# Low halves of weight blocks and of the gated output: from VectorE and GpSimd to VectorE alone

## The chip, the cores and the metric

The kernel runs on one core of a Trainium2 chip. Its engines each take their own instructions in a fixed order: TensorE (PE; its weight loads are listed as PEld), VectorE (DVE), ScalarE (ACT), GpSimd (POOL) and SyncE (SP), which here issues the DMAs. The metric is the device time of one execution in microseconds; the time of a kernel is the median over its runs.

## The reference

The reference is a decoder trunk of two layers on 2048 tokens of width 1024, all in float32. Cut to what matters:

```python
# layer A: gated MLP with causal mixing inside chunks of 128 tokens
u, v, z = split(h @ w_in, 3)                 # each 2048 wide
v = rms_norm(gelu(v), sgu_g)
mixed = einsum(tril(w_s), v) + b_s
y = gelu(u) * mixed * silu(z)                # the gated output
x = x + gate * (y @ w_out)
# shared k and v of three dilation groups (1, 4, 16)
k, v = split(h_kv @ w_kv, 2);  k = rms_norm(k, k_norm_g)
# layer B: dilated sliding-window attention, 24 query heads, three groups
q, z = split(h_b @ w_in_b);    q = rms_norm(q) * 128 ** -0.5
o = softmax-weighted sum over the groups of attention(q_g, k_g, v_g)
x = x + gate * ((o * silu(z)) @ w_out_b)
```

Each `h` is an RMS norm of x with a scale and shift computed from a conditioning vector.

## The kernel before

**Two halves of a number.** TensorE is fed a rounded format (`float32r`). To keep the precision, each operand is held as a high half, which is the rounded value, and a low half, which is the value less the high half. A product takes three matmuls: high by high, high by low, low by high (`mm3`, L262). So each weight block, 128 rows by 512 columns, is loaded raw by DMA, copied to its high half by ACT (L242) and subtracted to its low half (L246). The function `split` (L240) does this and chooses the engine of the subtraction: POOL where the caller says `pool`, or where a running count of blocks `wcnt` modulo `share[0]` is 3; else DVE. `wunits` (L248) makes the blocks of a dense product, `dense_f` (L285) those of the products whose output has features on the partitions. Raw blocks lie in 6 buffers, split ones in 8; a buffer comes free when its last reader is done, and SP issues loads in order.

**Stages.** The tokens are worked in four quarters of 512 (`for Q in range(NQ)`, L1197). Per quarter, `layer_A` (L648) computes v (four blocks of 512 columns, `dense`), u and z (eight blocks of 256 columns each, `dense_f`), and the output projection (`dense` over `yT`, L720). As z's blocks are done, L685 to L690 take silu, multiply into the gated output y, copy y's high half on ACT (L689) and subtract its low half (L690). `norm_T2` (L462) then makes the normalised, transposed operands of what follows; L715 to L717 compute each row's norm before it (L233 and L234 on POOL between them). `proj_B` (L738) computes shared k and v (`kv_block`, three blocks of 8 weight blocks), and q of three groups and layer B's z (`q_block`, `z_block`) with a Strassen scheme of seven products of four weight blocks each (`dense_s`, L361); L386 adds up the products on DVE. L780 to L783 norm q on POOL, and L785 stores it. `make_ops` (L487) makes the Strassen operands, with their low halves in turn on POOL and DVE (L496).

The weight blocks of one quarter are 32 for v, 32 for u, 32 for z, 32 for the output projection, 24 for kv and 112 for q and z of layer B. In `begin` (L580), which does the first v block of the first quarter, 8 blocks are made with `ordered=True`, which puts their low halves on POOL.

**Side work.** Attention of a quarter's blocks (`attend`, L1013, steps `att_1` to `att_4`) and other small work run as generators in a list `fillers`; `tick` (L84), called after each weight block of a dense product, advances them at `rate[0]` steps a tick, so their instructions lie between those of the dense products. `share[0]` is 4 at the start, is set very large at L1196 before the quarters begin, and back to 4 at L694, behind layer A's z of the first quarter. On POOL attention has the steps L941 to L944, L968 and L1043. `finish` (L1048) makes 16 weight blocks of its own whose low halves are subtracted on POOL at L1058.

**Order.** A planner of the framework orders each engine's instructions when the program is built, from the order of the source, the dependences and its own estimates of durations; only loads in `wunits` with `ordered` and what stands in `issue_after` are pinned. An engine waits in order: an instruction whose input isn't ready holds back all behind it.

Of the kernel before, what the change touches and what calls it, by code (L numbers as in the profile page):

```python
# [12 lines left out]
F32 = mybir.dt.float32  # L13
F32R = mybir.dt.float32r
AF = mybir.ActivationFunctionType
ALU = mybir.AluOpType
# [18 lines left out]
def trunk(ctx, tc, out, x, c, a_ada_w, a_ada_b, a_norm_g, a_w_in, a_sgu_g, a_w_spatial,  # L35
          a_b_spatial, a_w_out, kv_ada_w, kv_ada_b, kv_norm_g, w_kv, k_norm_g, b_ada_w,
          b_ada_b, b_norm_g, b_w_in, b_q_norm_g, b_w_out, dbg=None):
    nc = tc.nc
# [43 lines left out]
    rate = [0, 0]  # L82
# [11 lines left out]
    def evt(name, dt=F32):  # L94
        return ep.tile([P, 512], dt, tag="ev", name=name)

    def pst(name, tag="a"):
        return ps.tile([P, 512], F32, tag=tag, name=name)
# [126 lines left out]
    def bcast(src, nm):  # L225
        t = bp.tile([P, 512], F32, tag="bc", name=nm)
        nc.sync.dma_start(t, src.broadcast_to([P, 512]))
        return t


    def rstd_of(ssq, n, width, nm):
        t = sp.tile([P, 16], F32, tag="rs", name=nm)
        nc.gpsimd.tensor_scalar(t[:, 0:n], ssq, 1.0 / width, EPS, ALU.mult, ALU.add)  # L233
        nc.gpsimd.tensor_tensor(t[:, 0:n], t[:, 0:n], mhalf[:, 0:n], ALU.pow)  # L234
        return t

    wcnt = [0]
    share = [4]
# [27 lines left out]
    def dense(hs, w, n0, nm, evac):  # L266

        pts = {}
        for kh, (hh, hl) in enumerate(hs):
            us = wunits(w, kh * KT, n0, f"{nm}_{kh}_")  # L270
            for pr in range(2):
                for t in (2 * pr, 2 * pr + 1):
                    if kh == 0:
                        pts[t] = pst(f"pd_{nm}_{t}", "d")
                for k in range(KT):
                    for t in (2 * pr, 2 * pr + 1):
                        sl = slice(t * P, (t + 1) * P)
                        mm3(pts[t], hh[:, k, sl], hl[:, k, sl], us[k],
                            kh == 0 and k == 0, kh == len(hs) - 1 and k == KT - 1)
                    tick(0.25)  # L280
                if kh == len(hs) - 1:
                    for t in (2 * pr, 2 * pr + 1):
                        evac(t, pts[t])

    def dense_f(hh, hl, w, n0, nm, evac):  # L285

        pts = [pst(f"pd_{nm}_{i}", "d") for i in range(2)]
        for kk in range(0, KT, 4):
            for j in range(0, 4, 2):
                u = wp.tile([P, 2, 2, 256], F32R, tag="w", name=f"w_{nm}{kk + j}")  # L290
                raw = rp.tile([P, 2, 256], F32, tag="raw", name=f"raw_{nm}{kk + j}")
                nc.sync.dma_start(
                    raw, w[(kk + j) * P:(kk + j + 2) * P, n0:n0 + 256].rearrange("(k p) n -> p k n", p=P))
                split(u[:, 0], u[:, 1], raw)
                for k in (kk + j, kk + j + 1):
                    for i in range(2):
                        wh = u[:, 0, k % 2, i * P:(i + 1) * P]
                        wl = u[:, 1, k % 2, i * P:(i + 1) * P]
                        nc.tensor.matmul(pts[i], wh, hh[:, k, :], start=k == 0, stop=False)  # L299
                        nc.tensor.matmul(pts[i], wh, hl[:, k, :], start=False, stop=False)  # L300
                        nc.tensor.matmul(pts[i], wl, hh[:, k, :], start=False, stop=k == KT - 1)  # L301
                    tick(0.25)
        for i in range(2):
            evac(i, pts[i])
# [109 lines left out]
    def bigr(nm):  # L414
        return big.tile([P, KT, QT], F32R, tag="big", name=nm)
# [40 lines left out]
    def new_ops(nm):  # L456

        t = [big.tile([P, 2, 2, 4, 256], F32R, tag="big", name=f"ho{nm}{i}") for i in range(4)]
        return {n: (t[i // 2][:, i % 2, 0], t[i // 2][:, i % 2, 1])
                for i, n in enumerate(("11", "12", "22", "s1", "s2", "s3", "s4"))}  # L460
# [107 lines left out]
    def v_evac(Q, m, sqv, j):  # L568
        def ev(t, pt):
            mb = m[j // 2][:, t, (j % 2) * 512:(j % 2 + 1) * 512]  # L570
            nc.scalar.activation(mb, pt, AF.Gelu_apprx_tanh)
            jk = evt(f"jk{Q}_{j}_{t}")
            nc.scalar.activation(jk, mb, AF.Square, accum_out=sqv[t][:, j:j + 1])
        return ev
# [73 lines left out]
    def layer_A(Q, hA, m, sqv, j0):  # L648
        for j in range(j0, 4):
            dense([hA], a_w_in, AW + j * 512, f"v{Q}{j}", v_evac(Q, m, sqv, j))  # L650
        for t in range(TPQ):
            nc.vector.tensor_reduce(sqv[t][:, 15:16], sqv[t][:, 0:4], AX.X, ALU.add)
            rv = rstd_of(sqv[t][:, 15:16], 1, AW, f"rv{Q}_{t}")
            for h in range(2):
                nc.vector.tensor_scalar(m[h][:, t, :], m[h][:, t, :], rv[:, 0:1], None, ALU.mult)
        mt = [big.tile([P, KT, QT], F32, tag="big", name=f"mt{Q}_{h}") for h in range(2)]

        def mix(e):

            pm = pst(f"pm{Q}_{e}")  # L660
            for t in range(TPQ):
                nc.tensor.matmul(pm[:, t * P:(t + 1) * P], m[e // 8][:, t, (e % 8) * P:(e % 8 + 1) * P],
                                 wst[:, e // 2, :], start=True, stop=True)
            nc.vector.scalar_tensor_tensor(
                mt[e // 8][:, e % 8, :].rearrange("p (c t) -> p c t", t=P),
                pm.rearrange("p (c t) -> p c t", t=P), late["sgu"][:, e:e + 1],
                late["b_s"][:, e // 2, :].unsqueeze(1).broadcast_to([P, TPQ, P]), ALU.mult, ALU.add)

        for j in range(8):
            def ev(i, pt, j=j):  # L670
                e = 2 * j + i
                mix(e)
                u = evt(f"u{Q}_{e}")
                nc.scalar.activation(u, pt, AF.Gelu_apprx_tanh)
                nc.vector.tensor_tensor(mt[e // 8][:, e % 8, :], mt[e // 8][:, e % 8, :], u, ALU.mult)
            dense_f(*hA, a_w_in, j * 256, f"u{Q}{j}", ev)
        yT = []
        for j in range(8):
            if j % 4 == 0:
                yT.append((bigr(f"yh{Q}{j}"), bigr(f"yl{Q}{j}")))  # L680

            def ev(i, pt, j=j):
                e = 2 * j + i
                z = evt(f"z{Q}_{e}")
                nc.scalar.activation(z, pt, AF.Silu)  # L685
                y = mt[e // 8][:, e % 8, :]
                nc.vector.tensor_tensor(y, y, z, ALU.mult)
                yh, yl = yT[e // 8]
                nc.scalar.activation(yh[:, e % 8, :], y, AF.Copy)  # L689
                (nc.vector if e % 2 or Q == 0 else nc.gpsimd).tensor_tensor(yl[:, e % 8, :], y, yh[:, e % 8, :].bitcast(F32), ALU.subtract)  # L690
            dense_f(*hA, a_w_in, 2 * AW + j * 256, f"z{Q}{j}", ev)

        if Q == 0:
            rate[0], share[0] = 0, 4  # L694
        xts = []
        for t in range(TPQ):
            xt = xp.tile([P, D], F32, tag="xin", name=f"xr{Q}_{t}")
            nc.sync.dma_start(xt, x[(Q * TPQ + t) * P:(Q * TPQ + t + 1) * P, :])
            xts.append(xt)
        sq1 = [sp.tile([P, 16], F32, tag="sq1", name=f"sq1{Q}_{t}") for t in range(TPQ)]  # L700
        hk = (bigr(f"hkh{Q}"), bigr(f"hkl{Q}"))
        hb, keep = new_ops(f"b{Q}"), {}
        for n in range(2):
            gb = bcast(gd[0:1, n * 512:(n + 1) * 512], f"ga{Q}{n}")

            def ev(t, pt, n=n, gb=gb):
                s_ = slice(n * 512, (n + 1) * 512)
                tmp = evt(f"xo{Q}_{n}_{t}")
                nc.vector.tensor_tensor(tmp, pt, gb, ALU.mult)
                nc.vector.tensor_tensor(xts[t][:, s_], xts[t][:, s_], tmp, ALU.add)  # L710
                nc.scalar.activation(tmp, xts[t][:, s_], AF.Square, accum_out=sq1[t][:, n:n + 1])
                if n == 1:
                    tt = Q * TPQ + t
                    nc.sync.dma_start(x1d[tt * P:(tt + 1) * P, :], xts[t])
                    nc.vector.tensor_tensor(sq1[t][:, 2:3], sq1[t][:, 0:1], sq1[t][:, 1:2], ALU.add)  # L715
                    r = rstd_of(sq1[t][:, 2:3], 1, D, f"r_b{tt}")
                    nc.vector.tensor_scalar(xts[t], xts[t], r[:, 0:1], None, ALU.mult)  # L717
                    if t % 2 == 1:
                        norm_T2(xts[t - 1:t + 1], t // 2, hk, keep, f"b{Q}_{t}_")
            dense(yT, a_w_out, n * 512, f"o{Q}{n}", ev)  # L720
        return hk, hb, keep
# [519 lines left out]
```

## Time and profile before

| what | before |
|---|---|
| median of 3 runs | 3096.16 us (3093.24 to 3102.12) |
| profiled execution, its own time | 3093.31 us |
| span of its instructions | 3091.6 us |
| granted TensorE clock, mean | 0.989 |
| PE busy | 2983.4 us |
| DVE busy | 1946.4 us |
| ACT busy | 1627.1 us |
| POOL busy | 1207.0 us |
| low halves of weight blocks (L246) on DVE / on POOL | 808 / 248 |
| low halves of y (L690) on DVE / on POOL | 40 / 24 |

The page and the trace are of one execution. A group's row gives line, engine, operation, output from inputs, shape, how often, busy time and mean duration, then the idle time of the engine before it and what ended it. A row of waits gives who waited for whom, the total in us, how often, and the longest. A row of the timeline gives start, duration, engine, line, operation, and in brackets the idle time before it. In names, w is a split weight block, raw its raw load, yl a low half of y, pd a sum of a dense product in PSUM.

### The profile page before, as it was taken

The numbers are of one execution on the slowest core, as the hardware profiler recorded it, in microseconds if no ns is written. First come the engines' busy times: TensorE is split into PE (matmuls) and PEld (weight loads), VectorE is DVE, ScalarE is ACT, GpSimd is POOL, SyncE is SP. The second block draws the span as 40 slices with busy tenths as digits, with TensorE's granted clock in tenths as the row PEclk, the third lists the DMA queues.
The fourth block names the chain that finished last, engine by engine and source line by source line (L and its number), as shares of the span: only waits on it lengthen the run. The fifth ranks groups of instructions, "written<-read, shape, count | busy, mean of one in ns | idle before, by whom it ended". The sixth has DMA issues, their size and how long they took to land. (4 is left out here: it accounts for less than half of the span.)

```text
span 3091.6 us, 45182 instructions
## 1 busy us (share of the span) xinstructions
PE 2983.4 (97%) x14928; PEld 2496.1 (81%) x14928; DVE 1946.4 (63%) x3286; ACT 1627.1 (53%) x3324; POOL 1207.0 (39%) x1376
## 2 busy tenths in 40 slices
PE   6999999999999999999999999999999999999999
PEld 5788878778887878778888877788887788877887
DVE  6787466663567286655676376756575476767861
ACT  4323345566466255566465355565464367867540
POOL 4047135541135145733344145634354251244332
PEclk8999999999999999999999999999999999999999
DMA  7899546663433367743433356743433366678642
GB/s 233 264 312 343 163 142 212 218 216 117 148 103 99 99 222 226 241 155 123 126 108 103 125 178 209 241 152 120 126 104 105 117 194 208 224 242 283 232 160 95
DMA packets 343485, 547.80 MB, mean 177 GB/s; under 512 B 36074, under 2 KB 135628, under 8 KB 343252
## 3 DMA queue, kind: packets, MB, share of 16 engines
q1 hardware_dynamic: 343252, 544.93, 54.8%
q8 instruction: 118, 1.93, 0.3%
q14 instruction: 115, 0.94, 0.1%
HBM read 439.28 MB, written 105.52 MB: 176 GB/s over the span
## 5 line engine op out<-in xcount | busy, mean ns | idle before, releaser
L264 PE MATMUL pd_v<-w_v,hAh 128*128 128x512 f32 x1024 | 330.0, 403 | 1.2 <-ACT hAh L450 1.2
L264 PE MATMUL pd_o<-w_o,yh 128*128 128x512 f32 x1024 | 318.5, 391 | 0.0
L264 PE MATMUL pd_kv<-w_kv,hkh 128*128 128x512 f32 x768 | 243.1, 395 | 1.7 <-DVE w_kv L246 1.5
L264 PEld LDWEIGHTS pd_o<-w_o,yh 128*128 128x128 f32 x1024 | 192.7, 189 | 39.6
L264 PEld LDWEIGHTS pd_v<-w_v,hAh 128*128 128x128 f32 x1024 | 191.5, 193 | 40.7 <-issue 1.7
L933 ACT ACTIVATE pr<-pr,stat,rt 128x256 f32<-128x256 f32 (+1 forms) x320 | 177.4, 556 | 59.9 <-DVE stat L927 38.3
L299 PE MATMUL pd_u<-hAh,w_u 128*128 128x512 f32 x512 | 207.1, 404 | 0.0
L299 PE MATMUL pd_z<-hAh,w_z 128*128 128x512 f32 x512 | 205.4, 401 | 0.0
L264 PE MATMUL pd_v<-w_v,hAl 128*128 128x512 f32 x512 | 203.9, 398 | 0.0
L301 PE MATMUL pd_u<-hAh,w_u 128*128 128x512 f32 x512 | 201.1, 393 | 1.9 <-DVE w_u L246 1.8
L301 PE MATMUL pd_z<-hAh,w_z 128*128 128x512 f32 x512 | 201.1, 393 | 0.0
L300 PE MATMUL pd_z<-hAl,w_z 128*128 128x512 f32 x512 | 200.4, 391 | 0.0
L300 PE MATMUL pd_u<-hAl,w_u 128*128 128x512 f32 x512 | 200.3, 391 | 0.0
L264 PE MATMUL pd_o<-w_o,yl 128*128 128x512 f32 x512 | 199.7, 390 | 0.0
L242 ACT ACTIVATE w_o<-raw_o 128x512 fp32r<-128x512 f32 x128 | 79.9, 630 | 188.6 <-PE pd_o L264 136.4
L264 PEld LDWEIGHTS pd_kv<-w_kv,hkh 128*128 128x128 f32 x768 | 144.6, 189 | 36.3 <-DVE w_kv L246 6.2
L242 ACT ACTIVATE w_u<-raw_u 128x512 fp32r<-128x512 f32 x128 | 79.0, 630 | 162.7 <-PE pd_u L301 78.4
L994 PEld LDWEIGHTS po<-kv,pT 128*128 128x128 f32 x1200 | 149.0, 193 | 18.5 <-POOL pT L968 8.6
L994 PE MATMUL po<-kv,pT 128*128 128x128 f32 x1200 | 152.5, 277 | 10.1 <-POOL pT L968 7.9
L246 DVE TENSOR_TENSOR w_o<-raw_o,w_o 128x512 fp32r<-128x512 f32 x96 | 69.5, 725 | 140.0 <-ACT w_o L242 139.3
L264 PE MATMUL pd_kv<-w_kv,hkl 128*128 128x512 f32 x384 | 151.5, 395 | 0.0
L242 ACT ACTIVATE w_z<-raw_z 128x512 fp32r<-128x512 f32 x128 | 77.9, 625 | 132.2 <-PE pd_u L301 54.2
(690 smaller groups left out, 7990.5 us busy)
## 6 DMA issues: line engine op xcount, KB each, us to landing
raw_q<-in_b_w_in_dram SPq DMA_DIRECT2D x144, 256.0 KB, 3.7
raw_v<-in_a_w_in_dram SPq DMA_DIRECT2D x128, 256.0 KB, 3.7
raw_u<-in_a_w_in_dram SPq DMA_DIRECT2D x128, 256.0 KB, 2.8
raw_z<-in_a_w_in_dram SPq DMA_DIRECT2D x128, 256.0 KB, 3.1
raw_o<-in_a_w_out_dram SPq DMA_DIRECT2D x128, 256.0 KB, 2.7
qt<-qd SPq DMA_DIRECT2D x96, 260.0 KB, 3.8
raw_kv<-in_w_kv_dram SPq DMA_DIRECT2D x96, 256.0 KB, 2.8
od<-ot SPq DMA_DIRECT2D x96, 256.0 KB, 3.0
```

Of the source, the lines that this page charges most:

```text
L242: nc.scalar.activation(hi, src, AF.Copy)
L246: e.tensor_tensor(lo, src, hi.bitcast(F32), ALU.subtract)
L264: last_mm[0] = nc.tensor.matmul(pt, a, u[:, w, :], start=f, stop=e, skip_group_check=more)
L299: nc.tensor.matmul(pts[i], wh, hh[:, k, :], start=k == 0, stop=False)
L300: nc.tensor.matmul(pts[i], wh, hl[:, k, :], start=False, stop=False)
L301: nc.tensor.matmul(pts[i], wl, hh[:, k, :], start=False, stop=k == KT - 1)
L933: nc.scalar.activation(pr[:, i, :], pr[:, i, :], AF.Exp, bias=mneg[:, i:i + 1], scale=u["rt"][:, h:h + 1], accum_out=lsum[:, i:i + 1])
L994: nc.tensor.matmul(po[:, h * P:(h + 1) * P], u["pT"][h // hp][:, h % hp, j, :], u["kv"][:, j, kh, 1, :], start=j == 0, stop=j == nk - 1)
```

## The change

`share[0]` isn't set back to 4 behind the first quarter's z, so it keeps its large value to the end, and every low half that `split` makes from there on is on DVE. The low half of y is on DVE for all columns of all quarters; before, every second one was on POOL in quarters 1 to 3. The 8 blocks with `ordered` and the 16 of L1058 stay on POOL. The high halves stay on ACT.

```diff
--- before.py
+++ after.py
@@ layer_A, z of layer A @@
                 nc.scalar.activation(yh[:, e % 8, :], y, AF.Copy)
-                (nc.vector if e % 2 or Q == 0 else nc.gpsimd).tensor_tensor(yl[:, e % 8, :], y, yh[:, e % 8, :].bitcast(F32), ALU.subtract)
+                nc.vector.tensor_tensor(yl[:, e % 8, :], y, yh[:, e % 8, :].bitcast(F32), ALU.subtract)
             dense_f(*hA, a_w_in, 2 * AW + j * 256, f"z{Q}{j}", ev)
 
         if Q == 0:
-            rate[0], share[0] = 0, 4
+            rate[0] = 0
```

## The prediction

> **What bounds the kernel now.** I read the page's busy times first, then busy time by stage, then what TensorE waited for.
>
> ```profile
> PE 2983.4 (97%) x14928; PEld 2496.1 (81%) x14928; DVE 1946.4 (63%) x3286; ACT 1627.1 (53%) x3324; POOL 1207.0 (39%) x1376
> ```
> ```profile
> 341.00:2805.00 2464.00, 2402.57 (x11945) 2008.90 (x11944) 1530.35 (x2630) 1378.27 (x2747) 975.75 (x1179) 0.99 0.51 161
> ```
>
> In a row by stage the columns are stretch, length, busy time of PE, PEld, DVE, ACT and POOL, granted clock, DMA share, GB/s. TensorE bounds the kernel almost everywhere. The change acts only between about 341 us (first output-projection weights) and 2805 us (last z block), and TensorE has no record of work for 2464.00 - 2402.57 = 61.4 us of it. That, and the slow clock behind long gaps, is all the change can win. The list of TensorE's waits names the gaps (total us, times, longest):
>
> ```profile
> PE pp L961 <- POOL pr L944: 9.2, 6, 2.2
> PE pt_b L472 <- DVE xr L717: 8.2, 4, 2.0
> PE po L994 <- POOL pT L968: 7.9, 2, 4.8
> PE pd_z3bb L264 <- ACT w_z3b L242: 4.5, 2, 3.7
> PE pd_q10b L264 <- DVE st_q10u L386: 3.1, 1, 3.1
> PE pd_q20a L264 <- DVE st_q21w L386: 2.3, 1, 2.3
> PE pd_q00b L264 <- DVE st_q00u L386: 2.0, 1, 2.0
> PE pd_kv L264 <- DVE w_kv L246: 1.5, 2, 0.9
> ```
>
> Low halves (L246) themselves hardly appear: 1.5 us. TensorE waits for attention steps on POOL (L944, L968), for the normalised rows (L717) and for sums between products (L386). A long gap costs more than itself:
>
> ```profile
> 2364.00:2370.00 6.00, 1.16 (x5) 0.68 (x4) 6.00 (x6) 0.63 (x1) 5.84 (x5) 0.97 0.10 20
> 2370.00:2373.00 3.00, 3.00 (x12) 2.71 (x12) 1.31 (x3) 0.63 (x1) 1.31 (x1) 0.50 0.42 87
> ```
>
> After the gap of 4.8 us the next 3 us ran at half clock, 1.5 us more. The Trainium skill ("TensorE: Matmul & The Clock Gate", section "What's actually happening") says the same of a free-running window of 3413 ns, so that a gap shorter than it costs by luck; the two kv rows further down agree (0.97 and 1.00 after gaps of 2.0 us each).
>
> **The change, moved work.** The low halves and their durations, DVE and POOL, over the whole run, then in the first stage, then of one name (min/median/max ns), and the gated output's (L690):
>
> ```profile
> 0.00:3092.00 3092.00, 654.99 (x808) 348.87 (x248) 0.99 0.55 177
> ```
> ```profile
> 0.00:335.00 335.00, 84.72 (x92) 14.87 (x9) 0.97 0.87 287
> ```
> ```profile
> L246 DVE TENSOR_TENSOR w_q<-raw_q,w_q x108: 673/684/1782, 474.8 to 2742.1; 128x512 fp32r<-128x512 f32 x108
> ...
> L246 POOL TENSOR_TENSOR w_q<-raw_q,w_q x36: 1271/1294/1754, 476.9 to 2742.5; 128x512 fp32r<-128x512 f32 x36
> ```
> ```profile
> L690 POOL TENSOR_TENSOR yl<-mt,yh 128x512 fp32r<-128x512 f32 x24 | 39.4, 1649 | 3.4 <-ACT yh L689 2.4 <-PE pd_z L300 1.0
> ```
>
> There are 808 + 248 = 1056 low halves. The first eight on POOL are pinned there (`ordered`), and the code makes 96 in layer A of the first quarter; of the 960 after it every fourth is on POOL: 240. With 24 of L690, 264 instructions move. No DMA, copy on ACT or matmul is added.
>
> POOL loses 348.87 - 14.87 + 1.3 + 39.4 = 374.7 us (the nine of the first 335 us hold one that moves) and falls to 832 us, 27%. DVE gains 264 x 0.684 = 180.6 us before anything is given back.
>
> **What DVE gets back.** The same form takes 684 ns in the middle and up to 1782 on DVE: POOL's presence lengthens it. These are the operations with both inputs in SBUF that suffer beside L246:
>
> ```profile
> L687 DVE TENSOR_TENSOR mt<-mt,z 128x512 f32<-128x512 f32 x64 | 60.6, 979 | 29.9 <-ACT z L685 29.6
> L675 DVE TENSOR_TENSOR mt<-mt,u 128x512 f32<-128x512 f32 x64 | 58.9, 930 | 20.7 <-ACT u L674 17.3
> L690 DVE TENSOR_TENSOR yl<-mt,yh 128x512 fp32r<-128x512 f32 x40 | 46.5, 1193 | 6.0 <-PE pd_z L300 2.9 <-ACT yh L689 2.8
> ```
>
> Over 684 ns each: L246 654.99 - 808 x 0.684 = 102.3 us, L687 16.8, L675 15.1, L690 19.1: 153 us. How much of it the moved instructions cause isn't shown; the ends are 0 and 153. By their share of POOL's busy time (375 of 1207) it would be 48; they run right beside DVE's own low halves, so I take half, 76. Net DVE +105 us (27 to 181), 2051 us, 66%. The Trainium skill ("SBUF — State Buffer", section "Who interferes with whom") calls this a lock: a VectorE instruction with two SBUF inputs and a GpSimd one reading SBUF can't run together, the later waits for the whole of the other. By it a low half on POOL can cost DVE up to 1294 ns, more than the 684 of doing it itself, and net DVE time could fall. The trace goes that way, with 1782 - 684 = 1098 ns as the worst.
>
> **The terms on TensorE's path.**
>
> *(a) Rows normalised between the output projection and kv (8.2 us, four times 2.0).* On POOL and then DVE:
>
> ```profile
> 433.64 1.58 POOL L246 TENSOR_TENSOR w_kv<-raw_kv,w_kv 128x512 fp32r<-128x512 f32 x1 [8.53 <-ACT w_kv L242]
> 435.19 1.75 POOL L496 TENSOR_TENSOR hob<-st_b,hob 128x512 fp32r<-128x512 f32 x1
> ```
> ```profile
> 433.98 3.50 DVE L246 TENSOR_TENSOR w_kv<-raw_kv,w_kv 128x512 fp32r<-128x512 f32 x2
> 437.41 0.22 DVE L715 TENSOR_TENSOR sq<-sq 128x1 f32<-128x1 f32 x2
> ```
>
> L715 starts the chain that ends in L717, and stands behind two low halves that took 3.50 us beside POOL. With POOL's own taken in, three take 3 x 0.684 = 2.05: 1.4 us sooner, were POOL's L496 not to slow them. I take 5 us for the four. Ends: 8.2 + 2 x 1.5 of clock = 11 gained, and 4 x 0.684 = 2.7 lost if the third only queues in front.
>
> *(b) The step from z to the output projection (7.9 us in two).*
>
> ```profile
> 2361.74 5.09 POOL L690 TENSOR_TENSOR yl<-mt,yh 128x512 fp32r<-128x512 f32 x3
> 2366.80 1.71 POOL L246 TENSOR_TENSOR w_o<-raw_o,w_o 128x512 fp32r<-128x512 f32 x1
> 2368.46 1.17 POOL L968 TENSOR_TENSOR pT<-pT,dg 128x256 f32<-128x256 f32 x1
> ```
> ```profile
> 2362.25 5.13 DVE L690 TENSOR_TENSOR yl<-mt,yh 128x512 fp32r<-128x512 f32 x3
> 2367.30 0.41 DVE L967 TENSOR_TENSOR pT<-pp,pT 128x256 f32<-128x256 f32 x1
> ```
>
> Three of L690 on each engine take 5.1 us against each other; all six on DVE alone take 4.1, so L967 ends at 2366.7 instead of 2367.7, and L968 finds POOL free: it ends at about 2367.5, not 2369.6. That is 2.1 us, twice: 4.3. Ends: 0 and 7.9 + 2 x 1.5 = 10.9.
>
> *(c) Sums between products (3.1 + 2.3 + 2.0 and small ones) and the last z block (4.5).* DVE runs in order, and here it stood before a wait for POOL; SP, in order too, held weight loads behind stores waiting for POOL:
>
> ```profile
> 575.19 1.77 DVE L561 TENSOR_SCALAR x<-x,r_a 128x1024 f32<-128x1024 f32 x1 [4.75 <-POOL r_a L234]
> ```
> ```profile
> SPq L785 <- POOL s_q L780: 73.7, 40, 4.5
> ```
>
> One low half of 1.3 us less in POOL's queue at each of about five gaps: 6.5 gained. Ends: 12 + 2 x 1.5 = 15 gained; 5 lost, should DVE's added halves come in front of L386.
>
> *(d) L944 (9.2 us).* Mostly the chain's own service, taken as 1; ends 0 and 4.
>
> *(e) What DVE delays.* In the kv stage DVE is nearly full:
>
> ```profile
> 430.00:480.00 50.00, 47.90 (x210) 38.98 (x210) 43.70 (x55) 30.02 (x62) 24.94 (x21) 0.97 0.53 164
> 1093.00:1145.00 52.00, 48.35 (x213) 37.47 (x212) 48.65 (x67) 28.46 (x58) 20.86 (x18) 1.00 0.66 211
> ```
> ```profile
> 430.00:480.00 50.00, 15.94 (x15) 6.00 (x4) 0.97 0.53 164
> ```
>
> The second fence is L246 alone. Four more are 2.7 us; its excess is 15.94 - 15 x 0.684 = 5.7, half returned 2.8: about nothing, but the weights wanted there have no slack. I take 5 lost over the four quarters here and in the q and z blocks; ends 0 and 25 (below). Everywhere else a low half is hidden by matmuls: a kv or v weight block feeds 12 matmuls, and the first quarter's z stage already has every low half on DVE, with TensorE never idle:
>
> ```profile
> 254.00:341.00 87.00, 87.00 (x387) 72.08 (x386) 56.67 (x57) 35.63 (x61) 44.87 (x30) 1.00 0.93 312
> ```
>
> DVE is 65% busy there. If that cover went, a late half would cost its 0.684 us.
>
> **Sum.** -5 - 4.3 - 6.5 - 1 + 5 = -11.8 us. The profiled execution took 3093.31 us (span 3091.6), so 3081.5; it lies 2.9 under the median of the runs (3096.16), which gives 3084 for a new median.
>
> **The rivals.**
>
> *Nothing moves (3095).* For: TensorE is 97% busy and the largest gaps end in chains that only begin on POOL. The planner may put freed work behind other waits. Against: the contended rows in (a) and (b).
>
> *Much more is won (3068).* The terms (a) to (d) near their better ends, 11 + 10.9 + 15 + 4 = 41 with about two thirds reached, 28. For: POOL stands before most of the gaps. Against: L944 and L717 keep service of their own.
>
> *DVE becomes late: slower (3116).* In each quarter 4 halves in the kv windows and 14 in the last q and z blocks come on top of DVE's queue: 18 x 0.684 = 12.3 us, 49 in four quarters. If half of that reaches TensorE, in front of L246 and L386, it is 25 lost; with (a) to (d) all but kept (5 won), +20. It decides once DVE is busy for over 97% of a kv window; with nothing given back the second row would stand at 48.65 + 2.7 of 52, 99%. Against: half the excess there belongs to POOL. The Trainium skill ("Perfetto Trace Analysis", section "Optimizing Scalar/DVE Operations") speaks for this side, that a saturated DVE may be helped by handing work even to GpSimd, but warns in the same place that the two share a port; the 1782 ns rows agree with the warning.
>
> *It doesn't do what it says.* The eight pinned halves and the 16 of L1058 stay on POOL; that is in the counts above and changes nothing.
>
> **Chances.** Forecast (3076 to 3092) 0.42, nothing moves 0.19, much won 0.14, slower 0.25. About 0.3%, 9.3 us, is what a measurement here can tell from no change. Faster than 3086.9: 0.14 and 0.25 of the forecast, 0.39; within: the rest of the forecast, all of the second and 0.01 of the slower case, 0.37; slower: 0.24. The range 3066 to 3108 leaves out some 0.05 below and 0.13 above. The forecast's own range is 3076 to 3092.
>
> **What would show it.** DVE's low halves: 1048 with a mean near 700 ns instead of 811; 8 on POOL. L968 right behind L967, and its wait under 5 us in all. The waits for L717 near 0.7 us each. POOL near 832 us, DVE near 2051. Wrong would be: low halves still long (then other POOL work holds DVE), TensorE waiting for L246 or L386 for over 20 us in all, or DVE over 97% in the kv windows.

## The result and the profile after

The changed kernel takes 3057.71 us (median of 4 runs, 3056.2 to 3062.09) against 3098.96 us of the kernel before on the same chip: a ratio of 0.9873, with a 95% interval of 0.9858 to 0.9889. The forecast of 3084 us and its range from 3066 up were wrong: over three times as much was won as the sum of 11.8 us. The profiled execution after took 3056.2 us (span 3054.5), 37.1 us less than the one before. Times below come from several chips, on which the kernel before took 3093 to 3099 us, so each run is compared by its ratio to that; 0.001 is 3.1 us. The changed kernel's own interval is some 5 us to either side, and so every loss given below has at least that.

Busy times of the page after:

```profile
PE 2966.3 (97%) x14928; PEld 2487.1 (81%) x14928; DVE 2003.8 (66%) x3550; ACT 1632.3 (53%) x3324; POOL 835.4 (27%) x1112
```

POOL has lost 372 us and DVE gained 57. TensorE, with the same 14928 matmuls, is busy for 17 us less: it ran less often at half clock. The trace's record of the granted clock has, from 100 us to the end of the span, 49.6 us at half clock before and 22.4 after, so 24.8 against 11.2 us of time lost. (Before, the 3.1 us wait for L386 near 1261 us had such a stretch behind it, like the one that the prediction shows at 2370.)

The low halves (L246) after, DVE and POOL, over the whole run; one name; and the operations that had suffered beside POOL:

```profile
0.00:3092.00 3092.00, 765.31 (x1048) 13.56 (x8) 0.99 0.55 177
```
```profile
L246 DVE TENSOR_TENSOR w_q<-raw_q,w_q x144: 669/685/1783, 475.1 to 2710.1; 128x512 fp32r<-128x512 f32 x144
```
```profile
L687 DVE TENSOR_TENSOR mt<-mt,z 128x512 f32<-128x512 f32 x64 | 55.1, 893 | 27.9 <-ACT z L685 27.8
L675 DVE TENSOR_TENSOR mt<-mt,u 128x512 f32<-128x512 f32 x64 | 54.7, 865 | 16.5 <-ACT u L674 14.9
L690 DVE TENSOR_TENSOR yl<-mt,yh 128x512 fp32r<-128x512 f32 x64 | 49.1, 812 | 1.6 <-PE pd_z L300 1.4
```

A low half on DVE takes 730 ns in the mean, not 811. TensorE's waits after:

```profile
PE pp L961 <- POOL pr L944: 8.8, 6, 2.1
PE pt_b L472 <- DVE xr L717: 5.7, 4, 1.5
...
PE pd_z3bb L264 <- ACT w_z3b L242: 4.0, 2, 3.7
PE po L994 <- POOL pT L968: 3.5, 1, 3.5
PE pd_kv L264 <- DVE w_kv L246: 3.2, 4, 1.7
...
PE pd_u L301 <- DVE w_u L246: 2.3, 2, 1.8
...
PE pd_z0ba L264 <- DVE st_z0bu L386: 0.5, 1, 0.5
```

Of the waits for sums between products on DVE (L386), 12.1 us in twelve before, only 0.5 is left. The time by stages says the same more plainly. Layer B's dense work in each quarter runs from the first kv matmul to the next v block, in the last quarter to the final projection. The sum of the four stretches (length, then busy time by engine), before:

```profile
sum 1058.20, PE 1011.74 PEld 830.27 DVE 759.13 ACT 643.92 POOL 535.28; mean PE 252.93 PEld 207.57 DVE 189.78 ACT 160.98 POOL 133.82
```

After:

```profile
432.70:662.90 230.20, 225.17 (x1009) 184.36 (x1008) 176.58 (x273) 138.33 (x257) 84.74 (x136) 1.00 0.67 217
1091.20:1321.40 230.20, 226.74 (x1014) 184.65 (x1014) 185.87 (x291) 136.31 (x256) 85.85 (x136) 1.00 0.72 237
1764.40:1993.00 228.60, 224.62 (x1009) 184.52 (x1009) 175.30 (x274) 138.06 (x258) 84.08 (x136) 1.00 0.68 221
2431.40:2772.20 340.80, 323.86 (x1793) 272.25 (x1791) 250.65 (x526) 240.75 (x587) 92.14 (x142) 0.98 0.70 224
sum 1029.80, PE 1000.39 PEld 825.78 DVE 788.40 ACT 653.44 POOL 346.80; mean PE 250.10 PEld 206.45 DVE 197.10 ACT 163.36 POOL 86.70
```

28.4 of the 37.1 us are won here: 11.4 by the clock (PE's busy time) and 17.1 as less idle time, 46.5 down to 29.4. Of it the kv blocks have 6.9 us and the Strassen products of q and z 21.5. Layer A's stages of quarters 1 to 3 won another 10.9, the end 0.4; the first quarter's start lost 2.6.

So the question is why a quarter of the low halves on POOL, which TensorE hardly ever waited for, cost some 37 us.

### The profile page after: what moved, and what is told of

Its sections match the earlier page's. It is cut to its first block, busy times and chain, and to the rows that moved or that the text cites. A ratio compares the mean times of both kernels' runs of the same rounds, so it can differ in the third digit from the quotient of the medians.

```text
span 3054.5 us, 45283 instructions
## 1 busy us (share of the span) xinstructions
PE 2966.3 (97%) x14928; PEld 2487.1 (81%) x14928; DVE 2003.8 (66%) x3550; ACT 1632.3 (53%) x3324; POOL 835.4 (27%) x1112
## 5 line engine op out<-in xcount | busy, mean ns | idle before, releaser
L242 ACT ACTIVATE w_o<-raw_o 128x512 fp32r<-128x512 f32 x128 | 80.0, 630 | 195.0 <-PE pd_o L264 137.3
L246 DVE TENSOR_TENSOR w_o<-raw_o,w_o 128x512 fp32r<-128x512 f32 x128 | 89.9, 704 | 134.1 <-ACT w_o L242 133.4
L242 ACT ACTIVATE w_u<-raw_u 128x512 fp32r<-128x512 f32 x128 | 79.0, 630 | 164.1 <-PE pd_u L301 70.1
L941 POOL TENSOR_TENSOR dg<-pr,ident 128x256 f32<-128x256 f32 x76 | 57.4, 755 | 358.7 <-ACT pr L933 334.4
L242 ACT ACTIVATE w_z<-raw_z 128x512 fp32r<-128x512 f32 x128 | 78.4, 626 | 141.5 <-PE pd_z L301 61.1
```

What stands on the lines that cost most here:

```text
L242: nc.scalar.activation(hi, src, AF.Copy)
L246: e.tensor_tensor(lo, src, hi.bitcast(F32), ALU.subtract)
L941: nc.gpsimd.tensor_tensor(dg, prev, ident.unsqueeze(1).broadcast_to([P, hp, P]), ALU.mult)
```

## The experiments

The theories. *Time:* each low half keeps POOL for 1.3 us, and what stands behind it in POOL's queue comes late (norms of q, L780 to L783, and SP's stores of q, L785, with weight loads behind them in SP's queue). *Held blocks:* a raw block is free only when its subtraction is done; on POOL that is later, and the next load into one of six buffers starts later. *Lengthening:* POOL's wide reads make DVE's subtractions longer. *Order:* the planner draws another order, and the gain is luck. Losses below are against the changed kernel, by the difference of the ratios. Code is cut to the lines that matter.

### Which part of the change

`e1_share_only` moves only the 240 low halves of weight blocks (L690 as before), `e2_yl_only` only the 24 of L690.

```diff
@@ e1_share_only, against the changed kernel @@
-                nc.vector.tensor_tensor(yl[:, e % 8, :], y, yh[:, e % 8, :].bitcast(F32), ALU.subtract)
+                (nc.vector if e % 2 or Q == 0 else nc.gpsimd).tensor_tensor(yl[:, e % 8, :], y, yh[:, e % 8, :].bitcast(F32), ALU.subtract)
@@ e2_yl_only, against the changed kernel @@
-            rate[0] = 0
+            rate[0], share[0] = 0, 4
```

> The changed kernel with the low halves of y as before (every second one on POOL in quarters 1 to 3): only the 240 low halves of weight blocks have moved. Theory A (POOL's queue was in the way: chains that pass through POOL, and the stores and DVE work behind them, come sooner): 240 of the 264 instructions and 335 of the 375 us are gone from POOL, so most of the gain stays, 3060 to 3070 us, and the step from z to the output projection keeps its two waits of about 3 to 5 us for L968. Theory B (the two engines hold each other up, DVE's operations with two SBUF inputs are shorter): much the same, 3060 to 3070, with DVE's L246 near 730 ns. Theory C (the planner only drew a luckier order): no fixed share, anything between 3058 and 3099.

Measured: 3057.12 us, ratio 0.9888 (0.9866 to 0.991): all of the gain, within the intervals.

> The kernel before with only the 24 low halves of y moved to DVE; every fourth low half of a weight block stays on POOL. Theories A and B: the two waits for L968 at the step from z to the output projection (7.9 us and half a window of slow clock each, 1.7 us) shrink: 4 to 11 us won, 3088 to 3095. Theory C: no fixed share.

Measured: 3089.14 us, ratio 0.9988 (0.9972 to 1.0004): a gain of 4 us that can't be told from none. The waits for L968 fell from 7.9 to 4.3 us in all:

```profile
PE po L994 <- POOL pT L968: 4.3, 2, 2.2
```

### POOL loaded again, piece by piece

These runs leave the changed kernel's halves on DVE and give POOL something to do at the same 264 places (behind every fourth block's subtraction, and every second of L690), each time other pieces of what a low half on POOL is. In the cuts `extra` is filled behind the first quarter's z, `a` and `b` are the first columns of the raw block (or y) and of its high half, and the call behind L690 is left out.

```diff
@@ changed kernel, split @@
         e.tensor_tensor(lo, src, hi.bitcast(F32), ALU.subtract)
+        if extra and i % 4 == 3:
+            again(src, hi)
@@ again(src, hi): e3_pool_again @@
+        nc.gpsimd.tensor_tensor(src, src, hi.bitcast(F32), ALU.subtract)
@@ e4_pool_waits: one column of both @@
+        nc.gpsimd.tensor_tensor(spare[:, 0:1], a, b.bitcast(F32), ALU.subtract)
@@ e5_pool_holds: a column of hi, 128x8 constants to a power, a column of src @@
+        nc.gpsimd.tensor_tensor(spare[:, 0:1], b, b, ALU.subtract)
+        nc.gpsimd.tensor_tensor(spare[:, 0:8], spare[:, 8:16], mhalf[:, 0:8], ALU.pow)
+        nc.gpsimd.tensor_tensor(spare[:, 0:1], a, a, ALU.subtract)
@@ e6_dve_twice @@
+        nc.vector.tensor_tensor(src, src, hi.bitcast(F32), ALU.subtract)
```

> The changed kernel, and POOL subtracts again in place (raw less high half, written over the raw block, whose content nobody needs after) at each of the 264 places where it did before, after DVE's own subtraction; the output is the same. DVE keeps all the work, POOL has its old load, its old waits and its old reads. Theory A: POOL's queue is as long as before, so the gain goes: 3090 to 3105. Theory B: the holding up returns in full on a DVE with 181 us more of its own: 3095 to 3115. Theory C: nothing on the path has changed, 3058 to 3065.

Measured: 3122.9 us, ratio 1.0103 (1.0076 to 1.013), 71 us lost, and slower than before. That speaks against the order: with POOL loaded again the gain is gone. POOL's subtraction stands behind DVE's here, so the raw block is held for longer than in the kernel before, and DVE does all its work besides; so the 71 us aren't the price of the low halves alone.

> The changed kernel, and at each of the 264 places POOL subtracts one column (128x1) of the same raw block and high half into a spare column. POOL's in-order queue waits for the same copies on ACT as before, but the work is about 0.1 to 0.2 us instead of 1.3 and reads next to nothing. If the waits in POOL's queue were what cost (part of theory A): 3085 to 3100. If POOL's time of service or the reads beside DVE cost (the rest of A, and B): 3058 to 3068. Theory C: 3058 to 3065.

Measured: 3057.39 us, ratio 0.9886 (0.9858 to 0.9915). 4 us lost, which can't be told from none, with POOL busy 108 us longer (0.41 us at each place). POOL's waiting for ACT's high half in its queue, and a block held only that long, cost little or nothing; and 264 added instructions by themselves don't lose the gain.

> The changed kernel, and at each of the 264 places POOL does three small operations: one column of the high half (so it waits for ACT's copy as the removed subtraction did), a power over 128x8 of constants (about 1.1 us of service that reads next to nothing from SBUF), and one column of the raw block (so the raw buffer comes free only then). POOL has its old waits, about its old service time and its old hold on the raw buffers, but not the long reads of SBUF. If service in POOL's queue or late raw buffers cost (theory A without the waits, which the run with one column has ruled out): 3085 to 3125, as with POOL subtracting again. If the reads beside DVE cost (theory B): 3055 to 3068, with DVE's L246 still near 730 ns on average.

Measured: 3126.44 us, ratio 1.0099 (1.0078 to 1.0119), 70 us lost. Its powers were larger than meant (1.76 us), but they didn't lengthen DVE's operations. Page and low halves of this run (its L256 is L246):

```profile
PE 2988.1 (96%) x14928; PEld 2497.3 (80%) x14928; DVE 1982.8 (64%) x3550; ACT 1630.4 (52%) x3324; POOL 1471.8 (47%) x1905
...
L244 POOL TENSOR_TENSOR spare<-spare,mhalf 128x8 f32<-128x8 f32 x264 | 464.7, 1760 | 19.6
```
```profile
L256 DVE TENSOR_TENSOR w_q<-raw_q,w_q x144: 669/685/1785, 472.5 to 2767.6; 128x512 fp32r<-128x512 f32 x144
```

DVE is busy for less time than in the changed kernel (1982.8 against 2003.8), and still the whole gain and more is gone. A loss of this size needs no lengthening; but POOL is busy 636 us longer than in the changed kernel, and the change had taken off 372.

> The changed kernel, and DVE itself subtracts a second time in place (raw less high half, over the raw block) at each of the 264 places: 264 x 0.684 = 181 us more on DVE, POOL untouched. It prices 181 us of DVE time, what the change adds before anything is given back. If DVE had room (the change's load is hidden, theory A): 3057 to 3067. If DVE time is what the kernel feels at the tight stages, which theory B needs (POOL's 1.3 us of reading costs DVE more than the 0.68 us of doing it): 3075 to 3100.

Measured: 3098.04 us, ratio 1.0012 (1.0 to 1.0024), 43 us lost for 163 us more on DVE (2166.7). DVE's time isn't free either: at most about a quarter of it reaches the end. It is a bound and no price, as the second subtraction holds the raw block for longer too (SP waited for DVE's second subtraction 65.5 us for raw_o and 57.8 for raw_u).

### Time or held blocks

Three runs were meant to part these two by a power with and without the raw block read behind it, and gave no answer: nothing tied the power to its place.

```diff
@@ again: e10_pool_time_short (e11_pool_time_long: 0:8, 8:16) @@
+        nc.gpsimd.tensor_tensor(spare[:, 0:4], spare[:, 8:12], mhalf[:, 0:4], ALU.pow)
@@ again: e9_short_holds @@
+        nc.gpsimd.tensor_tensor(spare[:, 0:1], b, b, ALU.subtract)
+        nc.gpsimd.tensor_tensor(spare[:, 4:8], spare[:, 8:12], mhalf[:, 0:4], ALU.pow)
+        nc.gpsimd.tensor_tensor(spare[:, 0:1], a, a, ALU.subtract)
```

> On top of the changed kernel, as in the run in which POOL waits for the high half, raises a small tile of constants to a power and then reads one column of the raw block (3126 us, 2.4 us of POOL at each of 264 places), but with 128x4 numbers in the tile in place of 128x8: that power took 1.0 us alone, so POOL has about 1.0 + 2 x 0.2 = 1.4 us at each place, 1.3 to 1.5 us being what the low halves took it in the kernel before (264 x 1.4 = 370 us). DVE's own operations are not lengthened. If POOL's time in its queue, or the raw blocks that it holds, carried the whole gain, this comes out at the kernel before, 3090 to 3105 us. If it needs DVE's lengthening as well (34 to 120 us of DVE), it stays at the changed kernel's time up to half way, 3057 to 3075 us.

Measured: 3319.98 us, ratio 1.0725 (1.0696 to 1.0754).

> On top of the changed kernel, at the same 264 places POOL raises 128x4 constants to a power (1.0 us) and neither waits for anything nor reads the raw block: POOL's time alone, 264 us of it, without late release of a raw block. If POOL's time in its queue delays what stands behind it (the norms' powers, the subtractions of Strassen operands, the stores to DRAM), 3065 to 3090 us; if the raw blocks held back were the cost, 3057 us as the changed kernel, within 5 us.

Measured: 3314.53 us, ratio 1.0714 (1.0687 to 1.0742).

> The same with 128x8 constants, 1.76 us each, 465 us of POOL, again with no wait and no raw block held: 0.6 us less per place than the run at 3126 us, which waited and held as well. If POOL's time is what costs, 3085 to 3115 us, and more than the run with 1.0 us; if the held raw blocks are, 3057 us within 5 us as long as POOL stays under full, since nothing that loads weights waits for POOL.

Measured: 3475.6 us, ratio 1.1236 (1.121 to 1.1263). All 264 powers were drawn to the front of POOL's queue (first and last start in e10 at 10 and 319 us), where the first weights and operands of layer A stood behind them (in e11 to 479 us). Of e10, the powers:

```profile
L241 POOL TENSOR_TENSOR spare<-spare,mhalf x264: 1007/1008/1536, 10.0 to 318.8; 128x4 f32<-128x4 f32 x132
```

Its waits:

```profile
PE pd_v L272 <- POOL hAl L460: 141.9, 7, 44.5
PE pd_v L272 <- POOL w_v L252: 83.5, 4, 57.9
```

Layer B's stretches were 1033.5 us in e10, about those of the changed kernel. The times of these runs say nothing of the question.

In the next three the power overwrites the column that the read of the high half has just written, so that it stays in its place (in e13 from 333 to 2788 us).

```diff
@@ again: e13_time_short (e14_time_long: 0:8, 8:16) @@
+        nc.gpsimd.tensor_tensor(spare[:, 0:1], b, b, ALU.subtract)
+        nc.gpsimd.tensor_tensor(spare[:, 0:4], spare[:, 8:12], mhalf[:, 0:4], ALU.pow)
@@ e15_held: as e13, and @@
+        nc.gpsimd.tensor_tensor(spare[:, 0:1], a, a, ALU.subtract)
```

> On top of the changed kernel, at the 264 places POOL reads one column of the high half (0.2 us), then raises 128x4 constants to a power (1.04 us) into the place that it has just written, so that the power stays at its place in the queue. The raw block isn't read: DVE's subtraction alone frees it. 264 x 1.24 = 327 us of POOL. If POOL's time in its queue is what costs (at 240 low halves of about 1.4 us it cost 36 us), about 3080 to 3100 us. If the held raw blocks are what costs, 3057 us within 6 us. If DVE's lengthening is, 3057 us as well, since nothing lengthens it here.

Measured: 3077.16 us, ratio 0.9941 (0.9926 to 0.9956), 21 us lost by POOL's time alone. The reads of a column took 0.41 us in the mean and the powers 1.14, so POOL is busy 405 us longer than in the changed kernel and not 327:

```profile
PE 2972.6 (97%) x14928; PEld 2490.7 (81%) x14928; DVE 1989.8 (65%) x3550; ACT 1632.4 (53%) x3324; POOL 1240.0 (40%) x1641
```

> The same with 128x8 constants (1.7 us, so about 1.95 us at each place, 515 us in all), the raw block again free of POOL. POOL's time: 3100 to 3125 us, and above the run with 1.24 us. Held raw blocks: 3057 us within 6 us, against 3126 us for the run with 2.15 us and the raw block held.

Measured: 3097.35 us, ratio 1.0004 (0.9992 to 1.0015), 41 us lost: the loss grows with the time, by 20 us for 162 us more of POOL (1402.0).

> The run with 1.24 us of POOL at each place, and behind the power one column of the raw block is read (0.2 us): wait, 1.43 us of time and the block held to its end, the low halves' own size, without wide reads beside DVE. POOL's time: 3085 to 3105 us, 0 to 6 us above the run that doesn't hold. Held blocks: 3085 to 3105 us, but 25 us or more above the run that doesn't hold. DVE's lengthening: 3057 us within 8 us in both.

Measured: 3100.34 us, ratio 1.0015 (1.0001 to 1.0029), 44 us lost. That is another 23 us over e13, for a read of one column behind the power. Its page:

```profile
PE 2981.1 (96%) x14928; PEld 2493.8 (80%) x14928; DVE 1998.3 (64%) x3550; ACT 1631.2 (53%) x3324; POOL 1322.4 (43%) x1905
```

Not all of the 23 is for holding, since that read takes POOL's time too, 82 us in all. At e13's price (21 us for 405) these are worth some 4 us, at e14's (20 for 162) some 10: estimates, which leave 13 to 19 us for the held blocks. With the longer power the step is 29 us (e5 less e14, POOL busy 70 us longer). So the difference met neither of the two ranges that were set down for it, 0 to 6 and 25 or more: both theories hold, and time has the larger share of e15's 44. Layer B's stretches, e13:

```profile
sum 1051.70, PE 1004.27 PEld 826.20 DVE 783.16 ACT 652.43 POOL 552.38; mean PE 251.07 PEld 206.55 DVE 195.79 ACT 163.11 POOL 138.09
```

And e15:

```profile
sum 1074.50, PE 1013.27 PEld 831.76 DVE 783.38 ACT 651.15 POOL 597.53; mean PE 253.32 PEld 207.94 DVE 195.85 ACT 162.79 POOL 149.38
```

From 1029.8 over 1051.7 to 1074.5 us: 21.9 for e13's time and 22.8 for the read behind it, with DVE equally busy in both runs, and nearly all that the whole runs lose. How holding delays a load is to be seen in one place. In both runs a power of 4.34 us happens to stand on POOL in the first q product of the second quarter. SP's queue there in e13, then in e15 (start, duration):

```profile
1157.09 3.04 SPq L264 DMA_DIRECT2D raw_q12t<-wt  x6
1160.18 0.42 SPq L551 DMA_DIRECT2D x<-in_x_dram  x1
```
```profile
1161.45 7.30 SPq L265 DMA_DIRECT2D raw_q12t<-wt  x6
1168.80 0.42 SPq L552 DMA_DIRECT2D x<-in_x_dram  x1
```
```profile
SPq L265 <- POOL spare L243: 4.5, 1, 4.5
SPq L265 <- DVE w_q12t L256: 2.0, 3, 0.8
```

The same six loads take SP 3.04 us where DVE alone frees the blocks, and 7.30 where POOL must. The last fence has SP's waits in e15 between 1152 and 1173 us; 4.5 of them are for POOL, put down to L243, the instruction right behind the read of the raw block (L245, which ended at 1166.6). What it does to TensorE is less plain. In the same q block, some 15 us later, TensorE waits in e15 for DVE's sums L398 (L386 of the kernel before):

```profile
PE pd_q12a L276 <- DVE st_q12v L398: 2.2, 1, 2.2
```

This wait isn't in e13. The sums stand on DVE behind a low half of w_q whose high half came late (ACT at 1183.88); but the loads of w_q stand in SP's queue among stores of q (L799 at 1175.83 and 1179.82), which wait for POOL's norms. So which of the two causes made this wait isn't shown. Over the run SP waited in e15 for POOL's last read of a block, under two names, 252 us:

```profile
SPq L265 <- POOL spare L245: 151.9, 98, 7.7
...
SPq L304 <- POOL spare L245: 100.2, 33, 8.8
```

In the kernel before, the same waits stood in the list, at most 78.8 us for one name:

```profile
SPq L253 <- POOL w_o L246: 78.8, 32, 10.9
...
SPq L292 <- POOL w_u L246: 76.5, 22, 8.5
```

### Where, and how far

`e16_strassen_only` puts the quarter back on POOL in the Strassen products alone (112 blocks), `e17_projections_only` in v, u, z, o and kv alone (128).

```diff
@@ split, e16 (e17: "not four and") @@
-        e = nc.gpsimd if pool or i % share[0] == 3 else nc.vector
+        e = nc.gpsimd if pool or four and i % share[0] == 3 else nc.vector
@@ wunits (blocks of a Strassen product have nk = 4) @@
-            split(u[:, 0, :], u[:, 1, :], raw, ordered)
+            split(u[:, 0, :], u[:, 1, :], raw, ordered, nk == 4)
@@ layer_A, behind the first quarter's z @@
-            rate[0] = 0
+            rate[0], share[0] = 0, 4
```

> The changed kernel with every fourth low half back on POOL in the Strassen products alone (blocks of w_q and w_z, four in each product); the layer's own projections (v, u, z, o and kv) keep all on DVE. If the loss is that of DVE standing before a wait for POOL, and SP behind POOL, between Strassen products, most of the 36 us are back: 3080 to 3098 us. If it is spread as the blocks are, by share of the blocks (about a third to a half of the 240), 3068 to 3077 us. If it is in the projections, 3057 to 3062 us.

Measured: 3077.96 us, ratio 0.9941 (0.9926 to 0.9956), 21 us lost.

> The changed kernel with every fourth low half back on POOL in layer A's projections v, u, z, o and in kv (128 of the 240 blocks), and on DVE in the Strassen products. If the costs add, the other run having lost 20 us of 37, this loses the other 17: 3070 to 3080 us. If most of it needs POOL to be loaded in the Strassen products, 3057 to 3066 us. If layer A's long projections carry nothing (TensorE waited there for no low half in the kernel before), the cost is that of the 24 kv blocks alone, DVE's 48 us windows going back from 48.1 to 49.8 us: about 3 to 6 us, 3060 to 3064 us.

Measured: 3067.42 us, ratio 0.9907 (0.9891 to 0.9923), 11 us lost. Together 32 of the 39 that the ratios give for the whole change. By stages each loses where its own blocks are: in e16 the q and z stages take 749.9 us against 727.6 in the changed kernel, and kv 302.6 against 302.2; in e17 q and z take 730.9 and kv 308.3. (Before the change they were 749.1 and 309.1.)

These two runs also show that SP's waits are no price. SP waits for POOL to free a raw block 117 us in all in e16, which loses 21 us, and 291 us in e17, which loses 11 (22 us in the changed kernel). Nor does the total tell: for blocks that DVE or POOL had to free, SP waited 1013 us before the change and 927 after it. The list shows where POOL gives the blocks back, and not what that costs.

`e12_every_second` goes the other way: the kernel before with every second low half on POOL.

```diff
@@ e12, against the kernel before @@
-        e = nc.gpsimd if pool or i % share[0] == 3 else nc.vector
+        e = nc.gpsimd if pool or i % share[0] == share[0] - 1 else nc.vector
...
-            rate[0], share[0] = 0, 4
+            rate[0], share[0] = 0, 2
```

> The kernel before with every second low half of a weight block on POOL in place of every fourth (480 in place of 240, about 330 us more of POOL and 165 us less of DVE as its own rows count). If DVE's length bounds the kernel, this is faster than before, under 3090 us. If POOL's share of the low halves is what costs, the loss goes on: the 37 us of 240 blocks again or more, 3135 us or above.

Measured: 3116.35 us, ratio 1.0069 (1.0043 to 1.0095), with DVE at 1868.5 us. The second 240 cost 21 us where the first, with the 24 of L690, cost 39. That what DVE is spared gives some of it back would fit; it isn't shown.

`e7_operands_too`, and `e18_operands_again` once more, put the low halves of the Strassen operands (L496; the 28 of them that were on POOL) on DVE as well; `e8_all_low_halves` also those of L452 and L1058.

```diff
@@ make_ops (L496), e7 and e18 @@
-            e = nc.gpsimd if n[0] % 2 else nc.vector
+            e = nc.vector
```

> The changed kernel with the low halves of the Strassen operands (L496; every second one is on POOL, 28 in all) on DVE as well. They lie in the first kv block, where DVE is 87 to 91% busy and POOL's L496 stretches DVE's operations to 1266 ns on average. Theory B: DVE is relieved, the waits for L717 and for w_kv shrink from 5.7 and 3.2 us, 3048 to 3056. Theory A: DVE is later by 28 x 0.684 = 19 us over four quarters, POOL's queue isn't in the way there: 3056 to 3072.

Measured: 3050.68 us, ratio 0.9851 (0.9836 to 0.9866).

> The version with the low halves of the Strassen operands (24 subtractions of 128x512, on POOL in the changed kernel) on DVE as well, once more. If it is faster than the changed kernel, the ratio lies again at 0.985, below 0.9873, about 3048 to 3054 us; if the 7 us of the first time were a chance, 3055 to 3060 us.

Measured: 3051.23 us, ratio 0.9849 (0.9826 to 0.9872). Both medians lie 0.002 below the changed kernel's ratio, with intervals that overlap its own: probably some 7 us faster, and the fastest version tried. The kv stages take 295 us instead of 302.

> As the run before, and the low halves of layer A's operands in quarters 1 to 3 (L452, 24) and of the last weights (L1058, 16) on DVE too, so that POOL makes low halves only in the first stage. Theory B: a further 2 to 8 us, 3042 to 3052, mostly at the q and z blocks and the last z block. Theory A: POOL is at 27% already, no gain, DVE later: 3056 to 3080.

Measured: 3055.39 us, ratio 0.9878 (0.9857 to 0.9899): nothing further; the rest of POOL's low halves are as well where they are.

## Why the prediction was wrong

**What held.** TensorE's bound, the place where the gain lies, and the counts: 1048 low halves on DVE and 8 on POOL, POOL at 835 us (832 was said), their mean 730 ns. Relief: by the prediction's own four rows, L246's excess fell from 102.3 to 48.5 us, L687's from 16.8 to 11.3, L675's from 15.1 to 10.9, L690's from 19.1 to 5.3: 77 us given back, where 76 was taken. That a half was taken was a choice with no row behind it, so this agreement is luck. DVE's net is +57 and not +105: these four rows alone come to +103, as forecast, but the other rows of DVE, which the prediction left out, fall by 29 us together (L892, L927, L561 and others by 1 to 4 each), and 17 us more is overlap between the records of different lines. So POOL's presence cost DVE more, and in more places, than the prediction took.

**Step (c) failed: sums between products, -6.5.** The q and z stages gave 21.5 us, more than the better end of 15. The step counted one low half of POOL's queue at five gaps with a name in the list of waits. The loss was spread over every quarter (layer B's four stretches gave 5.3, 6.3, 7.5 and 9.3 us), and it came of the low halves of these very products: with them back on POOL (e16) the q and z stages are 22 us longer again. What POOL did there is what e13 to e15 show, time in its queue, with the chain of norms and SP's stores behind it, and raw blocks given back late. The prediction quoted a row for the first (L785) and none for the second, though SP's waits for POOL's L246 were in the trace. It went by the list of TensorE's waits, and that list puts a wait down to the last link, L386 or L242, and not to what made that link late. For layer A's stages of quarters 1 to 3, which gave 10.9, the sum held (b)'s 4.3.

**The clock was left out of the sum.** It stood in the ends alone ("x 1.5 of clock"), yet it is 13.6 of the 37 us: 13 stretches at half clock behind the first 100 us before, five after. The Trainium skill ("TensorE: Matmul & The Clock Gate", section "What's actually happening") has the gate close after an idle window of about 3.4 us. In the trace of before, twelve of the 13 stretches began within 5 us of the start of a gap of 1.8 to 4.8 us (the last lies at the kernel's end), and ten of these gaps were under 3.4 us, so the trace shows shorter gaps to cost as well. They don't always: of 16 gaps of 1.7 to 2.5 us eight had such a stretch behind them. A gap of 2 us should so have been priced at some 0.9 us more, half of the 1.7 that a stretch of 3.4 us loses (an estimate from these).

**(a) Rows before kv, -5.** L717's wait fell from 8.2 to 5.7 us, not to four times 0.7: 2.5 of the 5. No third low half has come in front of L715; there are two, as before (the next starts behind it at 440.02), and they take 2.40 us instead of 3.50:

```profile
437.56 2.40 DVE L246 TENSOR_TENSOR w_kv<-raw_kv,w_kv 128x512 fp32r<-128x512 f32 x2
439.88 0.22 DVE L715 TENSOR_TENSOR sq<-sq 128x1 f32<-128x1 f32 x2
```

Two low halves in a row take some 1.3 us elsewhere (1.29 in e13 at 1172 us). Here POOL's L496 runs beside them (437.74 to 439.40 us), as the prediction feared, and with L496 on DVE (e7) the kv stages take 7 us less again. In the change itself they gave 6.9.

**(b) From z to the output projection, -4.3.** The wait fell by 4.4, but that the size came out is luck. Without L690's move (e1) the wait fell as far, to 3.1, and with that move alone (e2) by 3.6; whether the time followed there can't be told, e2's gain being 4 us within 5. After the change the planner has L967 ahead of the six L690:

```profile
2340.24 0.41 DVE L967 TENSOR_TENSOR pT<-pp,pT 128x256 f32<-128x256 f32 x1
2340.57 0.68 DVE L246 TENSOR_TENSOR w_o<-raw_o,w_o 128x512 fp32r<-128x512 f32 x1
2341.17 4.23 DVE L690 TENSOR_TENSOR yl<-mt,yh 128x512 fp32r<-128x512 f32 x6
```

**(d)** gave 0.4 of 1. **(e) What DVE delays, +5.** TensorE's waits for L246 on kv blocks rose from 1.5 to 3.2 us, and a kv window is no nearer to full than before:

```profile
432.70:480.80 48.10, 46.09 (x209) 37.38 (x208) 41.94 (x60) 30.89 (x64) 18.70 (x17) 1.00 0.53 169
1091.20:1141.80 50.60, 47.34 (x212) 37.42 (x212) 46.14 (x71) 28.36 (x59) 14.58 (x14) 1.00 0.65 209
```

DVE is at 87% and 91% of them, not at 97. So the rival of a late DVE lacked its condition. Its mechanism may exist, at no more than a quarter of a microsecond per microsecond of DVE (e6); by that the 57 us cost 15 at most (an estimate from e6), and the whole of POOL's relief would be 37 to 52 us.

**The rival "much more is won" (3068)** named the right side, with a chance of 0.14. Its ends added to 41 us, and nearly all of it came, but not step by step: (a) and (b) stayed far below their ends of 11 and 10.9, and (c) went over its 15. Taking two thirds of the ends had no row behind it. "Nothing moves" fell with the result itself, and e13 to e15 say why: POOL's queue was in the way.

**What stays open.** How the change's 39 us divide. At e13's price the 372 us of POOL that it took off are worth some 19, and e15's step puts held blocks at 13 to 19 (estimates); what DVE's own 57 us take back is in the 39 too. How much DVE's lengthening costs by itself isn't shown: e15 loses 44 us without it, but has POOL busy 487 us longer than the changed kernel, where the low halves took 372; by the two prices above that makes 6 to 14 us of the 44 (an estimate). A wide read on POOL that holds no raw block would have told; no run has it.

## What to carry to other kernels

An engine at 39% busy can still cost 1.3%: what counts is what waits in its queue and which buffers it alone gives back. The waits of the engine that issues the loads show which buffers these are, though not their price; a run that gives the helper its time back, with and without the buffer, does. Moving short steps off a slow helper can pay even onto an engine that is busier (63% here), where they sit between a load and the release of its buffer. And an added instruction that depends on nothing may not stay where it was written: tie it to its neighbours before drawing a conclusion from it.

## What was not expected of the hardware

A power of small constants on POOL doesn't lengthen DVE's subtractions beside it. In e5 POOL spent 464.7 us on 264 of them. The 193 low halves on DVE that ran beside a power, and beside no other work of POOL, took 685 ns in the mean and 724 at most, and those with POOL idle 688. In e3, where POOL subtracted 264 times 128x512 again, the 167 low halves beside only such a subtraction took 1103 ns in the mean and up to 1790, and DVE's total rose by 123 us, 0.47 us each:

```profile
PE 2988.6 (96%) x14928; PEld 2498.7 (80%) x14928; DVE 2127.0 (68%) x3550; ACT 1625.2 (52%) x3324; POOL 1249.7 (40%) x1377
```

The Trainium skill ("SBUF — State Buffer", section "Who interferes with whom") has a VectorE instruction with two SBUF inputs contend with a GpSimd instruction that reads SBUF. The powers read SBUF too, so the trace agrees for the wide reads of e3 and not for the small ones of e5, although these last as long (1.64 us in the median, e3's subtractions 1.61).

The power itself is dear for its size: in the median 1.01 us for 128x4 numbers (e10) and 1.64 us for 128x8 (e5), against 1.29 us for a subtraction of 128x512 (w_q in the kernel before).
